# One of the two operands of each VectorE instruction of a state-space layer moved to PSUM, and the banks dealt out anew

## The chip, the cores and the metric

The kernel runs on one core of a Trainium2 chip. The metric is device time in microseconds (us) of one execution. Five engines work side by side, each through its own queue in order: PE (TensorE, matmuls), DVE (VectorE), ACT (ScalarE), POOL (GpSimd) and SP (SyncE, which here only issues DMAs). They meet at semaphores. SBUF is the on-chip memory of tiles; PSUM is a smaller one of eight banks, into which PE writes, and which DVE and ACT read and write too. In this kernel a bank is 128 x 512 float32, and every PSUM tile is called `b`.

## The reference

A decoder trunk over 256 tokens of 2048 channels in float32: one state-space (S5) layer and a SwiGLU, one dilated attention layer and a SwiGLU, each behind an RMS norm. Only the S5 part is touched:

```
dt = exp(log_dt);  mag = exp(lam_re * dt);  ang = lam_im * dt
lam = mag * (cos ang + i sin ang)                 # 128 groups x 64 states, complex
f   = (lam - 1) * conj(lambda) / |lambda|^2
x_t = lam * x_(t-1) + f * B u_t                   # a scan over the 256 tokens
y_t = Re(C x_t) + d_skip * u_t
z   = gelu(y);  out = val(z W) * sigmoid(gate(z W))
```

## The kernel before

**Two parts.** The first 188 us of the span are the S5 layer; the rest is a stream of large matmuls (lines 717, 718 and 721) over glu, the two SwiGLUs and attention, with PE as its bound. The stream begins when the last scan result has gone through PE.

**The S5 layer.** Tokens are taken in 64 chunks of four, the 128 groups in 64 pairs, and the pairs in four quarters k = 0 to 3 of 16 pairs. Its steps, in the order in which DVE meets them:

- Parameters (`s5_params`): some 72 small DVE instructions, mostly 128x64, one after another: exp of a step, sine and cosine by polynomials, the first four powers of lam (`by`, three instructions of `cmul` each), the coefficients of W. Operands and results lie in SBUF tiles (named `hi`, `lo` and `scr` here, since small vectors are packed in larger tiles).
- `s5_chunk_powers` on POOL: powers 1 to 4 of lam^4, in a small SBUF tile (`cp`).
- `w_build` on DVE: W for all quarters, 128x256 pieces with the coefficients `g` in PSUM bank 7. PE transposes them (`v_trans`), ACT copies them to `wpad`, PE multiplies with the tokens (`v_build`), ACT copies the result into `vs`, the 64 states per chunk.
- The scan over `vs` in three kinds of levels, each of the form dst += a^c * src: `l1` within blocks of four chunks (three levels of 128x512 or 128x480 instructions), `l2` across the 15 blocks for 32 pairs at once (14 steps of four 128x64 instructions, each step reading the one before), `l3` from the blocks to their chunks (three levels of 128x480). One level is four DVE instructions (lines 504 to 507): two products (of the state and of the state with its planes swapped), a sum, a sum back into `vs`. `pipe` sets the products of one level between the sums of the last, `go(ops, others)` spreads one list of instructions between another's.
- DVE's order: `l1([0, 1])`; `l2(0)` with `l1([2])` spread between; `l3(0)`; `l2(1)` with `l3(1)` spread between; `l3(2)`; half-size levels of quarter 3. POOL does `l1([3])`, the last level of quarter 3, and `q_build` (Q = C lam^t) in its own queue beside it.
- PE: `t_part(k)` (32 matmuls, the part of y that comes from the tokens of the same chunk) and `s_part(k)` (64 matmuls of line 581 onto the same banks, from the states), then ACT's gelu, then `z_part(k)`: eight transposes, an ACT copy (`hi` part) and two DVE subtractions (`lo` part) that give the stream its operand.

**What sets the order.** All of it is the order in which the program is written: each engine executes its instructions in that order, with semaphore waits that the framework derives from reads and writes of tiles. The products of the levels go to `t1p` (bank 6, and `za` or `hi` tiles in SBUF) and `dtmp` (SBUF); the coefficients come from `cp` in SBUF.

Of the kernel before, what the change touches and what calls it, by code (L numbers as in the profile page):

```python
# [32 lines left out]
def constants():  # L33
    """Identity, channel mask, selections of token rows, and the three attention masks."""
# [21 lines left out]
def layouts(i):  # L56
    """The inputs as the program reads them: copies in another order, nothing else."""
# [42 lines left out]
class Trunk:  # L100
# [50 lines left out]
    # ------------------------------------------------------------------ setup  # L151
# [39 lines left out]
    def s5_load(self):  # L191
# [7 lines left out]
        # planes of B: (Br, -Bi, -Br) times the gain; of C: (-Ci, Cr, Ci)  # L199
# [7 lines left out]
        # Q of two quarters of the pairs, a block for each g2: (slot, g2, t, c, re/im, q)  # L207
# [24 lines left out]
    def cmul(self, eng, out, ar, ais, x, xs, t1, t2):  # L232
        """out = a x for planes (re, im): ar twice, ais = (-im a, im a), xs = (im, re) of x."""
        eng.tensor_tensor(t1, ar, x, ALU.mult)
        eng.tensor_tensor(t2, ais, xs, ALU.mult)
        eng.tensor_tensor(out, t1, t2, ALU.add)

    def s5_params(self, rms):
        """Powers of the transition, and the coefficients of W."""
        nc, small = self.nc, self.small  # L240
# [16 lines left out]
        pio.append(lambda: tt(den, lr, lr, mul))  # L257
# [32 lines left out]

        tt(lam[:, 0, 1:3], bc(mag, S3, [1]), pp.rearrange("p (r q) -> p r q", r=2), mul)
# [4 lines left out]
        by(lam[:, 1:2, 1:3], lam[:, 0, 1], lam[:, 0, 2], lam[:, 0:1], 1)  # L296
        # f = (lam - 1) conj(lambda) / |lambda|^2
        u1, u2 = [v.rearrange("p (r q) -> p r q", r=2) for v in (ap_, az)]
        tt(u1, bc(lr, S3, [1]), nr[:, 0:2], mul)
        ts(lam[:, 1, 0], lam[:, 1, 2], -1.0, None, mul)  # L300
        tt(u2, bc(li, S3, [1]), nr[:, 1:3], mul)
        tt(u1, u1, u2, add)
        by(lam[:, 2:4, 1:3], lam[:, 1, 1], lam[:, 1, 2], lam[:, 0:2], 2)
        tt(fx, u1, bc(den, S3, [1]), mul)
# [5 lines left out]
        by(g[:, 2::-1], fx[:, 0], fx[:, 1], lam[:, 0:3], 3)  # L310

    def s5_chunk_powers(self, eng):
        """Powers 1..4 of conj(lam^4): re, and (im, -im) of conj, for the chunk recurrence."""
        mul = ALU.mult
        lam = self.lam
        sm = [self.small(w, True) for w in (192, 192, 128, 192, 192, 128)]
        cp = self.cp = [sm[i].rearrange("p (r q) -> p r q", r=3) for i in (0, 1, 3, 4)]
        tmp = self.ctmp = [sm[i].rearrange("p (r q) -> p r q", r=2) for i in (2, 5)]
        # plane 0: re; planes 1, 2: (b, -b) where a = re - i b
# [15 lines left out]
    def zv(self, k, hl):  # L335
        """A part of z^T of four K tiles."""
        c = 2048 * (k % 2) + 1024 * hl
        return self.zt[k // 2][:, c:c + 1024].rearrange("p (k t) -> p k t", k=4)

    def s5(self, st):  # L340
# [16 lines left out]
        # 1 / rms of the tokens: by rows, then for every (g2, j, c) in the partitions  # L357
# [5 lines left out]
        # B with the gain of u, conjugate  # L363
# [3 lines left out]
        # d_skip times the gain on the diagonal of the kernel of lag 0  # L367
# [44 lines left out]
        def q_build(k, ts):  # L412
            """Planes (re, im) of Q_t = C lam^t, t = 1..4, of 16 pairs."""
# [17 lines left out]
        def w_build(k, q0, n):  # L431
            """W_j = lam^(3-j) f B of n pairs (conjugate), in [(g2,p), q, re/im, j, c]."""
# [20 lines left out]
        def v_build(u):  # L453
            """The states that the chunks add, of 8 pairs."""
# [15 lines left out]
        def k_build(k):  # L470
            """K[3-j] = Re(C lam^(3-j) f B) of 16 pairs in [(k // 2, j, c), q, g2, c']."""
# [10 lines left out]
        def t_tile(t, n):  # L482
            """A blank tile for T of n pairs: (g2, j'), q, c'."""
# [5 lines left out]
        def t_build(t, h, bs):  # L489
            """T[j, j'] = K[j' - j]: the rows of K moved by 16 (3 - j') partitions, of 16 or 32 pairs."""  # L490
# [6 lines left out]
        def level(k, src, dst, ns, coef, eng, n, q0=0, nq=16):  # L497
            """slots dst += a^coef * slots src, nq pairs."""
# [5 lines left out]
            return [lambda: eng.tensor_tensor(ta, bc(cp[coef][:, 0, qs], sh, [1, 1]), x, mul),  # L504
                    lambda: eng.tensor_tensor(tb, bc(cp[coef][:, 1:3, qs], sh, [1]), x[:, :, ::-1, :], mul),  # L505
# [52 lines left out]
        # Y = U T + S Q, z = gelu(Y), transposed and split  # L558
# [561 lines left out]
```

## Time and profile before

| | |
|---|---|
| median of 3 timed runs | 2275.83 us (2275.25 to 2276.38) |
| span of the profiled execution | 2274.4 us |
| PE busy | 2157.1 us, 95% |
| DVE busy | 1591.5 us, 70% |
| ACT busy | 1034.1 us, 45% |
| POOL busy | 207.4 us, 9% |
| mean granted TensorE clock | 0.985 |

The span runs from the first to the last instruction of the profiled execution; it lies 1.4 us under the median of the timed runs. The shares are means over two unlike parts: in the S5 part (up to 188.4 us) DVE is busy for 175 us and PE for 89, and after it PE for nearly all of the time. "Held" in what follows means that an instruction's recorded time is longer than that of the same instruction elsewhere.

### The profile page before, as it was taken

To read this page: it belongs to the slowest core of one execution; us is meant where nothing else is said; L and a number is where in the kernel's file an instruction comes from. 1 tells how busy PE (TensorE), PEld (TensorE's weight loads), DVE (VectorE), ACT (ScalarE), POOL (GpSimd) and SP (SyncE) were. 2 spreads that over 40 slices of the span, in tenths; PEclk is the share of its full clock that TensorE was granted. 3 is DMA by queue.
4 is the path that set the end of the run, shared out by engine and by line. 5 is a ranking of instruction groups with operands and counts; after the bars stand their busy time and mean duration, and the time that the engine had idled before them with its cause. 6 is when DMAs were issued, how large, how long until landed. Compare 5 with 4: busy or idle time off the path is not lost.

```text
span 2274.4 us, 27357 instructions
## 1 busy us (share of the span) xinstructions
PE 2157.1 (95%) x10520; PEld 1793.2 (79%) x10520; DVE 1591.5 (70%) x2646; ACT 1034.1 (45%) x1173; POOL 207.4 (9%) x166
## 2 busy tenths in 40 slices
PE   2639999999999999999999999999999999999998
PEld 2628888888888888878888888887888888888886
DVE  9995677677677766484777677677776776675544
ACT  4503444544444444343545555545444444443443
POOL 7930000000000000000000000000000000000000
PEclk9869999999999999999999999999999999999999
DMA  5324545555555555545555444445555555555553
GB/s 183 90 84 163 189 185 193 209 191 185 204 185 191 199 196 192 200 173 199 195 185 184 146 154 166 148 167 185 187 191 199 194 192 199 189 204 203 194 195 130
DMA packets 60563, 410.37 MB, mean 180 GB/s; under 512 B 7248, under 2 KB 8144, under 8 KB 12816
## 3 DMA queue, kind: packets, MB, share of 16 engines
q1 hardware_dynamic: 58176, 400.13, 48.8%
q10 hardware_dynamic: 1968, 6.92, 0.9%
q8 instruction: 82, 1.34, 0.2%
q0 software_dynamic: 288, 1.57, 0.2%
q14 instruction: 49, 0.40, 0.0%
HBM read 398.90 MB, written 2.10 MB: 176 GB/s over the span
## 4 chain that ended last, share of the span: by engine, by line
PE 87%; DVE 10%; issue 1%; ACT 1%; DMA 0%; ACTq 0%; DVEq 0%
PE b L718 28%; PE b L717 28%; PE b L721 28%; DVE scr L787 2%; DVE scr L137 1%; DVE lo L137 1%; PE b L149 1%; DVE dtmp L505 1%; PE b L581 1%; DVE vs L507 1%; PE b L1010 1%; DVE vs L137 1%; ACT hi L695 1%; DVE raw L137 1%; PE b L1041 1%
## 5 line engine op out<-in xcount | busy, mean ns | idle before, releaser
L146 DVE SCALAR_TENSOR_TENSOR lo<-raw,gcol,hi 128x1024 fp32r<-128x1024 f32 x464 | 594.6, 1291 | 325.2 <-ACT hi L699 319.2
L717 PE MATMUL b<-hi,xt 128*128 128x512 f32 x1856 | 726.6, 391 | 1.5 <-ACT hi L699 1.3
L718 PE MATMUL b<-lo,xt 128*128 128x512 f32 x1856 | 723.1, 390 | 0.9 <-DVE lo L146 0.9
L699 ACT ACTIVATE hi<-raw,gcol 128x1024 fp32r<-128x1024 f32 x464 | 525.2, 1148 | 399.3 <-PE b L721 376.5
L721 PE MATMUL b<-hi,xt 128*128 128x512 f32 x1856 | 572.3, 390 | 0.0
L137 DVE TENSOR_TENSOR lo<-raw,hi 128x1024 fp32r<-128x1024 f32 x272 | 335.8, 1240 | 301.5 <-ACT hi L695 300.0
L695 ACT CAST hi<-raw 128x1024 fp32r<-128x1024 f32 x272 | 283.5, 1052 | 315.3 <-PE b L721 305.9
L717 PEld LDWEIGHTS b<-hi,xt 128*128 128x128 f32 x1856 | 349.0, 188 | 73.5 <-ACT hi L699 1.8
L718 PEld LDWEIGHTS b<-lo,xt 128*128 128x128 f32 x1856 | 348.9, 188 | 72.8 <-DVE lo L146 1.8
L721 PEld LDWEIGHTS b<-hi,xt 128*128 128x128 f32 x1856 | 348.7, 188 | 73.0
L718 PE MATMUL b<-lo,ht 128*128 128x512 f32 x704 | 274.3, 390 | 2.5 <-DVE lo L137 2.5
L717 PE MATMUL b<-hi,ht 128*128 128x512 f32 x704 | 274.0, 389 | 0.1
L787 DVE STREAM_TRANSPOSE scr<-scr 32x128 f32<-32x128 f32 x704 | 212.9, 302 | 11.3
L721 PE MATMUL b<-hi,ht 128*128 128x512 f32 x704 | 217.1, 389 | 0.0
L718 PEld LDWEIGHTS b<-lo,ht 128*128 128x128 f32 x704 | 132.2, 188 | 31.4 <-DVE lo L137 4.1
L717 PEld LDWEIGHTS b<-hi,ht 128*128 128x128 f32 x704 | 132.2, 188 | 27.8 <-ACT hi L695 0.5
L721 PEld LDWEIGHTS b<-hi,ht 128*128 128x128 f32 x704 | 132.2, 188 | 27.5
L791 POOL TENSOR_TENSOR ht<-scr,ht 128x512 fp32r<-128x512 f32 x44 | 57.1, 1297 | 880.8 <-ACT ht L790 852.4
L790 ACT CAST ht<-scr 128x512 fp32r<-128x512 f32 x44 | 27.3, 621 | 178.6 <-DVE scr L787 178.6
L791 POOL TENSOR_TENSOR xt<-scr,xt 128x512 fp32r<-128x512 f32 x20 | 25.9, 1297 | 830.6 <-ACT xt L790 725.2
L718 PE MATMUL b<-lo,z 128*128 128x512 f32 x256 | 100.1, 391 | 0.6 <-DVE lo L137 0.6
L787 DVE STREAM_TRANSPOSE scr<-x 32x128 f32<-32x128 f32 x320 | 96.8, 302 | 4.9
(210 smaller groups left out, 1605.0 us busy)
## 6 DMA issues: line engine op xcount, KB each, us to landing
raw<-in_fi SPq DMA_DIRECT2D x176, 1024.0 KB, 4.8
raw<-in_fo SPq DMA_DIRECT2D x88, 1024.0 KB, 4.8
raw<-in_wq SPq DMA_DIRECT2D x48, 1024.0 KB, 4.8
raw<-in_glu SPq DMA_DIRECT2D x32, 1024.0 KB, 4.8
raw<-in_wo SPq DMA_DIRECT2D x16, 1024.0 KB, 4.8
raw<-in_kv SPq DMA_DIRECT2D x8, 1024.0 KB, 4.8
qp<-in_xr SPq DMA_DIRECT2D x4, 512.0 KB, 11.0
xw<-in_xu SPq DMA_DIRECT2D x4, 512.0 KB, 11.5
```

What stands on the lines that cost most here:

```text
L137: self.nc.vector.tensor_tensor(out, in0, in1, op)
L146: self.nc.vector.scalar_tensor_tensor(out, in0, s, in1, op0, op1)
L149: self.nc.tensor.transpose(out, in_, self.ident[:n, :n])
L505: lambda: eng.tensor_tensor(tb, bc(cp[coef][:, 1:3, qs], sh, [1]), x[:, :, ::-1, :], mul),
L695: nc.scalar.copy(hi, raw)
L699: nc.scalar.activation(hi, raw, AF.Copy, scale=gk)
L717: nc.tensor.matmul(ps[b], xh, hi[:, c], start=first, stop=False)
L718: nc.tensor.matmul(ps[b], xh, lo[:, c], start=False, stop=False)
L721: nc.tensor.matmul(ps[b], xl, hi[:, c], start=False, stop=last)
L787: nc.vector.transpose(out[32 * q:32 * q + 32, :, 32 * a:32 * a + 32], src[32 * a:32 * a + 32, :, q, :])
L790: nc.scalar.copy(dst(0), out)
L791: nc.gpsimd.tensor_tensor(dst(1), out, dst(0).bitcast(F32), ALU.subtract)
```

## The change

The text of the program changes in the S5 functions alone. Parameters: `n, p, dt, mag, den, kk, app, pp, low, t1, nr, fx` move to PSUM banks 0 to 3 (`ps`), the others stay in SBUF; the two squares of |lambda|^2 go from DVE to ACT; |angle| is taken by two shifts in place of a minimum; two copies (`low`) are added. Chunk powers: `cp` stays in SBUF for POOL, and ACT copies it to two banks (`coefs`, banks 7 and 5), from which DVE reads. Products: `t1p` is banks 6 and 4 for all DVE levels; in `l2` the first product goes to the bank that holds the coefficients. Banks: `kk` takes 0 and 1, `t_part` 2 and 3 or 0 and 1, `z_part(0)` 7 and 2. Order: `t_part(2)` and `t_part(3)` come after `s_part(1)`, and the two subtractions of `z_part(0)` come before `l3(2)`.

```diff
+        homes = [[self.bank(i), 0] for i in (0, 1, 2, 3)]
+        ins = self.small
...
+        t, r = ins(64), ins(64)
+        n, p, dt, mag = [ps(64) for _ in range(4)]
+        zz, mags, k2, ang, l2, dens = [ins(64) for _ in range(6)]
+        den, kk = ps(64), ps(64)
+        ap_, az = ins(128), ins(128)
+        app, pp = ps(128), ps(128)
+        nc.scalar.activation(den, lr, AF.Square)
+        nc.scalar.activation(l2, li, AF.Square)
         for f in self.exp_steps(dt, ldt, t, n, r, p):
             f()
...
-        pio.append(lambda: tt(den, lr, lr, mul))
+        pio.append(lambda: tt(den, den, l2, add))
...
+        low = ps(256).rearrange("p (k r q) -> p k r q", k=2, r=2)
+        t1, t2 = ps(384), ins(384)
...
+        nc.vector.tensor_copy(low[:, 0], lam[:, 0, 1:3])
...
         def level(k, src, dst, ns, coef, eng, n, q0=0, nq=16):
...
-            return [lambda: eng.tensor_tensor(ta, bc(cp[coef][:, 0, qs], sh, [1, 1]), x, mul),
-                    lambda: eng.tensor_tensor(tb, bc(cp[coef][:, 1:3, qs], sh, [1]), x[:, :, ::-1, :], mul),
+            a_ = cp[coef][:, :, qs]
+            if eng is dve:
+                a_ = cps[k // 2][:, coef, :, 16 * (k % 2) + q0:16 * (k % 2) + q0 + nq]
+            return [lambda: eng.tensor_tensor(ta, bc(a_[:, 0], sh, [1, 1]), x, mul),
+                    lambda: eng.tensor_tensor(tb, bc(a_[:, 1:3], sh, [1]), x[:, :, ::-1, :], mul),
...
+        def coefs(h, b):
+
+            v = self.bank(b)
+            cps[h] = v[:, 0:384].rearrange("p (k r q) -> p k r q", k=4, r=3)
+            tl2[h] = [w.rearrange("p (r q) -> p r q", r=2) for w in (v[:, 384:448], self.ctmp[:, 64 * h:64 * h + 64])]
+            nc.scalar.copy(cps[h], self.cpa[:, :, :, 32 * h:32 * h + 32])
...
-            ta, tb = ta4[0][:, h], ta4[1][:, h]
+            ta, tb = tl2[h]
+            a_ = cps[h][:, 3]
...
-        t1p = [t1p[0], za[:, 1024:1536]]
+        coefs(0, 7)
+        coefs(1, 5)
         go(l1([0, 1], dve))
...
-        py = [t_part(0, tz, 32), t_part(1, tz, 32), t_part(2, tq[0], 16)]
+        py = [t_part(0, tz, 32), t_part(1, tz, 32)]
...
-        lo = z_part(0)
+        lo = z_part(0, (7, 2))
         l31 = l3(1)
         go(l2(1), l31)
-        py.append(t_part(3, tq[1], 16))
+        go(lo)
+        s_part(1, py[1])
+        py += [t_part(2, tq[0], 16), t_part(3, tq[1], 16)]
         next(st)
-        s_part(1, py[1])
...
         s_part(2, py[2])
-        go(lo)
```

DVE at the start of the parameters, before. `hi_84` is the tile of the inputs, `hi_108` that of small vectors, both in SBUF:

```order
L143 TENSOR_SCALAR hi_84<-hi_84 128x64 [waits DMAHW1_49]
L143 TENSOR_SCALAR hi_108<-hi_84 128x64 [waits DVE_49]
L141 TENSOR_SCALAR hi_108<-hi_108 128x64 [waits DVE_49] x2
L146 SCALAR_TENSOR_TENSOR hi_108<-hi_108,hi_84 128x64
L141 TENSOR_SCALAR hi_108<-hi_108 128x64 [waits DVE_49]
```

And of the changed kernel, where `b_129` is bank 0 of the parameters:

```order
L143 TENSOR_SCALAR hi_84<-hi_84 128x64 [waits DMAHW1_49]
L143 TENSOR_SCALAR hi_108<-hi_84 128x64 [waits DVE_49]
L141 TENSOR_SCALAR b_129<-hi_108 128x64 [waits DVE_49,Activation_49]
L141 TENSOR_SCALAR hi_108<-hi_108 128x64 [waits DVE_49]
L146 SCALAR_TENSOR_TENSOR hi_108<-b_129,hi_84 128x64
L141 TENSOR_SCALAR hi_108<-hi_108 128x64 [waits DVE_49]
```

The third instruction now writes to PSUM, and it has a wait on ACT that it did not have. What it waits for stands in ACT's queue of the changed kernel (L377 are the squares of the token rows, L393 the gain of B, L259 and L260 the two squares of |lambda|^2, the first into the same bank `b_129`):

```order
L377 ACTIVATE qp,ss<-qp 128x1024 [waits DMAHW7_49]
L393 ACTIVATE z_86<-z_86 128x16x64 [waits DMAHW3_49,Pool_49]
L259 ACTIVATE b_129<-hi_84 128x64 [waits DMAHW1_49]
L260 ACTIVATE hi_108<-hi_84 128x64
L398 ACTIVATE r<-r 128x2 [waits DVE_49]
```

The two squares stand behind all four row squares and the gain of B.

DVE where `l1` ends and `l2(0)` begins, before (`scr_106` and `scr_107` hold powers, `vs` the states, `b_242` is bank 6):

```order
L504 TENSOR_TENSOR b_242<-scr_106,vs 128x512 [waits Activation_49]
L137 TENSOR_TENSOR scr_107<-scr_107,vs 128x64 [waits DVE_49,Pool_49]
L137 TENSOR_TENSOR scr_107<-scr_107,vs 128x64 [waits Pool_49]
L137 TENSOR_TENSOR scr_107<-scr_107,vs 128x64 [waits DVE_49]
L137 TENSOR_TENSOR vs<-scr_107 128x2x32 [waits DVE_49]
L137 TENSOR_TENSOR scr_107<-scr_107,vs 128x64 [waits DVE_49]
```

And in the changed kernel, where `b_765` is bank 7 and `b_767` bank 5:

```order
L523 TENSOR_TENSOR b_250<-b_767,vs 128x512 [waits Activation_49]
L137 TENSOR_TENSOR b_765<-b_765,vs 128x64 [waits DVE_49]
L137 TENSOR_TENSOR scr_106<-b_765,vs 128x64 [waits DVE_49,Pool_49]
L137 TENSOR_TENSOR b_765<-b_765,vs 128x64 [waits DVE_49]
L137 TENSOR_TENSOR vs<-b_765,scr_106 128x2x32 [waits DVE_49]
L137 TENSOR_TENSOR b_765<-b_765,vs 128x64 [waits DVE_49]
```

Each instruction has one operand in a bank, and the second product of a step now waits for the first, since both name the same bank.

ACT of the changed kernel where the states are finished (L480 are the last copies of `v_build` into `vs`, L551 the copies of the coefficients into the banks, L501 the blank tile for `t_build`). In the kernel before, the L480 rows are L464, and the L501 rows (there L485) follow them directly:

```order
L480 COPY vs<-b_720 128x8x63 [waits PE_49]
L480 COPY vs<-b_738 128x8x63 [waits PE_49]
L648 DMA xw<-in_cd 128x1024 [waits DMAHW5_49,DMAHW1_49]
L551 COPY b_765<-scr_107 128x384 [waits DVE_49,Pool_49]
L551 COPY b_767<-scr_107 128x384
L501 COPY tz<-vs 128x2048 [waits Activation_49]
```

The copy that the first `l1` instruction reads (it has a wait on ACT) is the last but two of this list, behind every copy of `v_build`.

## Rows read from the trace of the kernel before

**Rows 1.** Stretches of the S5 layer, one row each: the stretch in us, its length, then for PE, weight loads, DVE, ACT and POOL the busy time and the instructions in brackets, then granted TensorE clock, DMA share and GB/s.

```profile
66.20:95.00 28.80, 25.92 (x486) 23.96 (x484) 28.77 (x25) 17.76 (x22) 28.01 (x19) 1.00 0.37 98
95.00:138.00 43.00, 4.57 (x48) 3.96 (x43) 42.16 (x70) 5.49 (x3) 33.65 (x26) 0.58 0.16 40
145.00:162.20 17.20, 11.53 (x110) 10.37 (x112) 16.44 (x68) 3.64 (x5) 0.00 (x0) 0.80 0.47 136
162.20:173.40 11.20, 7.11 (x62) 6.40 (x58) 11.10 (x14) 1.20 (x2) 6.30 (x4) 0.80 0.41 169
173.40:188.40 15.00, 14.99 (x128) 14.21 (x128) 8.92 (x20) 3.80 (x5) 0.00 (x0) 0.89 0.13 43
```

**Rows 2.** PE in order of time from `s_part(0)` to the first matmul of the stream; in brackets the idle time before and what ended it.

```profile
145.03 7.79 PE L581 MATMUL b<-qp,vs 128*64 128x128 f32 x64 [40.21 <-DVE vs L507]
...
154.10 1.97 PE L567 MATMUL b<-raw,xw 128*64 128x128 f32 x32
161.60 7.71 PE L581 MATMUL b<-qp,vs 128*64 128x128 f32 x64 [5.54 <-DVE vs L507]
173.41 7.79 PE L581 MATMUL b<-xw,vs 128*64 128x128 f32 x64 [4.11 <-DVE vs L507]
180.91 7.63 PE L581 MATMUL b<-qp,vs 128*64 128x128 f32 x64
188.47 0.50 PE L717 MATMUL b<-hi,z 128*128 128x512 f32 x1
```

**Rows 3.** The small instructions of `l2(0)`, grouped, from 95 to 138 us, with POOL busy for most of it: count, busy us and mean ns, idle before.

```profile
L137 DVE TENSOR_TENSOR scr<-scr,vs 128x64 f32<-128x64 f32 x42 | 22.3, 572 | 0.3
L137 DVE TENSOR_TENSOR vs<-scr 128x64 f32<-128x64 f32 x14 | 10.4, 742 | 0.4
```

**Rows 4.** The same of `l2(1)`, from 145 to 162.2 us, with POOL idle.

```profile
L137 DVE TENSOR_TENSOR scr<-scr,vs 128x64 f32<-128x64 f32 x42 | 7.4, 219 | 0.3
L137 DVE TENSOR_TENSOR vs<-scr 128x64 f32<-128x64 f32 x14 | 3.1, 224 | 0.4
```

**Rows 5.** POOL in order of time, early in `l1`: start, length, engine, line, operation, tiles (out<-in).

```profile
66.45 1.60 POOL L236 TENSOR_TENSOR hi<-lo 128x512 f32<-128x512 f32 x1
68.13 1.59 POOL L234 TENSOR_TENSOR lo<-scr,z 128x512 f32<-128x512 f32 x1
69.68 1.74 POOL L235 TENSOR_TENSOR lo<-scr,z 128x512 f32<-128x512 f32 x1
```

**Rows 6.** DVE in order of time beside POOL's rows of the group before.

```profile
66.85 1.75 DVE L505 TENSOR_TENSOR dtmp<-scr,vs 128x512 f32<-128x512 f32 x1
68.53 0.69 DVE L506 TENSOR_TENSOR b<-b,vs 128x512 f32<-128x512 f32 x1
69.13 1.14 DVE L504 TENSOR_TENSOR z<-scr,vs 128x512 f32<-128x512 f32 x1
70.19 0.68 DVE L507 TENSOR_TENSOR vs<-b,dtmp 128x512 f32<-128x512 f32 x1
```

**Rows 7.** ACT in order of time: the gain of B (line 377 before, 393 after).

```profile
16.02 1.04 ACT L377 ACTIVATE z<-z 128x1024 f32<-128x1024 f32 x1
```

**Rows 8.** DVE in order of time in the parameters, and the first instruction of `w_build` (last row).

```profile
6.43 2.03 DVE L141 TENSOR_SCALAR hi<-hi 128x64 f32<-128x64 f32 x2
8.38 0.22 DVE L146 SCALAR_TENSOR_TENSOR hi<-hi,hi 128x64 f32<-128x64 f32 x1
...
11.98 4.66 DVE L141 TENSOR_SCALAR hi<-hi 128x64 int32<-128x64 int32 x2
16.56 2.39 DVE L146 SCALAR_TENSOR_TENSOR hi<-hi 128x64 f32<-128x64 f32 x3
18.87 0.18 DVE L141 TENSOR_SCALAR hi<-hi 128x64 f32<-128x64 f32 x1
...
29.07 0.43 DVE L137 TENSOR_TENSOR b<-b,z 128x256 f32<-128x256 f32 x1
```

**Rows 9.** The last POOL instruction before the chunk powers (d_skip on the diagonal), beside the parameters.

```profile
16.94 1.92 POOL L371 TENSOR_TENSOR lo<-cst,hi 128x1024 f32<-128x1024 f32 x1
```

**Rows 10.** ACT in order of time where `v_build` ends: the last two copies into `vs`; in brackets the idle time before and what ended it.

```profile
74.73 1.96 ACT L464 COPY vs<-b 128x504 f32<-128x504 f32 x2 [0.36 <-PE b L460]
```

**Rows 11.** DVE in order of time at the start of `l3(2)`.

```profile
162.25 0.66 DVE L504 TENSOR_TENSOR hi<-scr,vs 128x480 f32<-128x480 f32 x1
162.82 1.65 DVE L505 TENSOR_TENSOR dtmp<-scr,vs 128x480 f32<-128x480 f32 x1
```

**Rows 12.** The first step of `l2(1)` in order of time (two products and a sum, the sum back into `vs`, the next product).

```profile
145.59 0.49 DVE L137 TENSOR_TENSOR scr<-scr,vs 128x64 f32<-128x64 f32 x3
146.11 0.23 DVE L137 TENSOR_TENSOR vs<-scr 128x64 f32<-128x64 f32 x1
146.37 0.23 DVE L137 TENSOR_TENSOR scr<-scr,vs 128x64 f32<-128x64 f32 x1
```

**Rows 13.** DVE instructions of 256 columns in order of time: two operands and the result in SBUF; one operand in a bank; the sum of two products, one of them in a bank.

```profile
25.72 0.42 DVE L236 TENSOR_TENSOR scr<-lo 128x256 f32<-128x256 f32 x1
...
29.41 0.41 DVE L137 TENSOR_TENSOR dtmp<-b,z 128x256 f32<-128x256 f32 x1
...
30.41 0.58 DVE L137 TENSOR_TENSOR raw<-b,dtmp 128x256 f32<-128x256 f32 x1
```

**Rows 14.** POOL in order of time: the last piece of `q_build`.

```profile
128.63 1.27 POOL L236 TENSOR_TENSOR raw<-z 128x512 f32<-128x512 f32 x1
```

More of the change, by code (lines that the diff above doesn't have):

```diff
@@ L238, in s5_params @@
     def s5_params(self, rms):
-        nc, small = self.nc, self.small
+        nc = self.nc
         tt, ts, stt = self.tt, self.ts, self.stt
@@ L243, in s5_params, with ps @@
         I = lambda v: v.bitcast(I32)
-        lr, li, ldt = self.par[:, 0:64], self.par[:, 64:128], self.par[:, 128:192]
-        t, n, r, p, dt, zz = [small(64) for _ in range(6)]
+        homes = [[self.bank(i), 0] for i in (0, 1, 2, 3)]
+        ins = self.small
+        def ps(w):
+            h = next(h for h in homes if h[1] + w <= 512)
+            h[1] += w
+            return h[0][:, h[1] - w:h[1]]
+        lr, li, ldt = self.par[:, 0:64], self.par[:, 64:128], self.par[:, 128:192]
+        t, r = ins(64), ins(64)
[6 more added lines that the diff above has]
+        nc.scalar.activation(l2, li, AF.Square)
         for f in self.exp_steps(dt, ldt, t, n, r, p):
             f()
-        mag = small(64)
         tt(zz, lr, dt, mul)
         e_ops = self.exp_steps(mag, zz, t, n, r, p)
-        ang, k2, kk = [small(64) for _ in range(3)]
-        ap_, az, pp = [small(128) for _ in range(3)]
-        den = small(64)
         pio = []
@@ L295, in s5_params @@
         nc.vector.tensor_copy(nr[:, 1], lam[:, 0, 2])
-        by(lam[:, 1:2, 1:3], lam[:, 0, 1], lam[:, 0, 2], lam[:, 0:1], 1)
-        u1, u2 = [v.rearrange("p (r q) -> p r q", r=2) for v in (ap_, az)]
+        by(lam[:, 1:2, 1:3], low[:, 0], lam[:, 0:1], 1)
+        u1, u2 = [v.rearrange("p (r q) -> p r q", r=2) for v in (app, az)]
         tt(u1, bc(lr, S3, [1]), nr[:, 0:2], mul)
         ts(lam[:, 1, 0], lam[:, 1, 2], -1.0, None, mul)
+        nc.vector.tensor_copy(low[:, 1], lam[:, 1, 1:3])
         tt(u2, bc(li, S3, [1]), nr[:, 1:3], mul)
         tt(u1, u1, u2, add)
-        by(lam[:, 2:4, 1:3], lam[:, 1, 1], lam[:, 1, 2], lam[:, 0:2], 2)
-        tt(fx, u1, bc(den, S3, [1]), mul)
+        by(lam[:, 2:4, 1:3], low[:, 1], lam[:, 0:2], 2)
+        tt(fx, u1, bc(dens, S3, [1]), mul)
         ts(lam[:, 2:4, 0], lam[:, 2:4, 2], -1.0, None, mul)
@@ L309, in s5_params @@
         nc.vector.tensor_copy(g[:, 3], fx)
-        by(g[:, 2::-1], fx[:, 0], fx[:, 1], lam[:, 0:3], 3)
+        by(g[:, 2::-1], fx, lam[:, 0:3], 3)
     def s5_chunk_powers(self, eng):
@@ L315, in s5_chunk_powers @@
         lam = self.lam
-        sm = [self.small(w, True) for w in (192, 192, 128, 192, 192, 128)]
-        cp = self.cp = [sm[i].rearrange("p (r q) -> p r q", r=3) for i in (0, 1, 3, 4)]
-        tmp = self.ctmp = [sm[i].rearrange("p (r q) -> p r q", r=2) for i in (2, 5)]
+        sm = [self.small(w, True) for w in (768, 128, 128)]
+        self.cpa = sm[0].rearrange("p (k r q) -> p k r q", k=4, r=3)
+        cp = self.cp = [self.cpa[:, i] for i in range(4)]
+        tmp = [v.rearrange("p (r q) -> p r q", r=2) for v in sm[1:]]
+        self.ctmp = sm[1]
         eng.tensor_copy(cp[0][:, 0:2], lam[:, 3, 1:3])
@@ L561, in t_part @@
         def t_part(k, tz, nq):
-            py = [self.bank(2 * (k % 3) + g2) for g2 in range(2)]
+            py = [self.bank(2 - 2 * (k % 2) + e) for e in range(2)]
             for e in range(2):
@@ L585, in s_part, with z_part @@
             zs[k] = z.rearrange("p j i g c -> p j (i g c)")
-        def z_part(k):
+        def z_part(k, bs=(7, 6)):
             zf, lo = zs[k], []
@@ L591, in z_part @@
             for e in range(2):
-                pt = self.bank(7 - e)
+                pt = self.bank(bs[e])
                 for j in range(4):
@@ L622, in s5 @@
                 q_build(u // 4, ((u - 1) % 4, u % 4))
-        t1p = [t1p[0], za[:, 1024:1536]]
+        coefs(0, 7)
+        coefs(1, 5)
         go(l1([0, 1], dve))
-        kk = [self.bank(4 + b) for b in range(2)]
+        kk = [self.bank(b) for b in range(2)]
         for b in range(2):
@@ L644, in s5 @@
         go(l2(0), l1([2], dve))
-        t1p = [stage[0][0][:, 512 * c:512 * c + 512] for c in range(2)]
         q_build(2, range(4))
```

31 lines of the change are left out of this document (15 added, 16 removed).

## The prediction

> **What bounds the kernel now.** I read the stretches first. In the S5 layer DVE is busy almost without a gap (28.77 of 28.80 us, 42.16 of 43.00), while PE has little to do between 95 and 138 us [rows 1]; the stream starts when the last `s_part` has ended, at 188.47 [rows 2]. So a microsecond that DVE saves before the last level is a microsecond of the whole, as long as DVE stays the one that is late. The stream behind it is not touched.
>
> Then I looked at why DVE is busy. The stretch 95 to 138 and the stretch 145 to 162.2 do the same work (70 and 68 instructions), but the first takes 43 us and has POOL at work for 33.65 of them, the second takes 17.2 with POOL idle [rows 1]. Grouped, the same 42 small instructions have a mean of 572 ns in the one and 219 in the other, the 14 sums 742 and 224 [rows 3, 4]. In order of time it can be seen what does it: at 66.85 a product of two SBUF tiles is recorded with 1.75 us and ends at 68.60, just after a POOL instruction has ended at 68.05; the sum behind it, with one operand in a bank, takes 0.69 although POOL runs from 68.13 to 69.72; so does the sum into `vs` at 70.19, 0.68 beside POOL's 69.68 to 71.42; the next product of two SBUF tiles, at 69.13, takes 1.14 and again ends after POOL has [rows 5, 6]. An instruction with two SBUF operands is held until the running POOL instruction ends, one with a bank among its operands is not, whether its result goes to a bank or to SBUF. The change gives each of them a bank, so I expect the hold to go. What it adds are two waits on ACT and some inside DVE.
>
> **The change part by part** (times of the profiled execution, span 2274.4; the runs' median is 1.4 more).
>
> *Parameters: a loss of 4.4 us.* The third DVE instruction now writes bank 0, where ACT's square of lam_re goes first, and that square stands behind ACT's gain of B, which ends at 16.02 + 1.04 = 17.06 [rows 7]. With some 0.2 for the square, DVE goes on at about 17.2, where it was at 6.43 [rows 8]. Its fourth instruction still reads and writes SBUF alone, as the pair at 6.43 which took 2.03 for two, so POOL's instruction of 16.94 to 18.86 [rows 9] holds it: 18.9. The rest ran in 11.98 - 8.38 = 3.6 us, then five instructions that were held from 11.98 to 18.87 and that cost some 0.7 without the hold, then 29.07 - 18.87 = 10.2 [rows 8]: 14.5 us. That gives 33.4, and two more instructions 33.5: `w_build` starts 33.5 - 29.07 = 4.4 late. The bounds: if the fourth isn't held, 2.8; if each of the 74 instructions costs 0.02 more for its bank, 5.9. I take 4.4. From here on everything is 4.4 later; `w_build` already has a bank in every product and keeps its length, so it ends at 66.2 [rows 1] + 4.4 = 70.6.
>
> *The copy of the coefficients: 11 us of waiting.* The first `l1` instruction now reads bank 7, which ACT fills behind its last copy into `vs`. That copy ended at 74.73 + 1.96 = 76.69 [rows 10], and as it is fed by `w_build` it moves to 81.1. The new copy (128x384, some 0.5 by the rate of the 128x504 ones) makes it 81.6. DVE stands still from 70.6 to 81.6, and all its later work is queued behind that wait. If that copy were early, nothing; so 0 to 11, and I take 11, since the order of ACT leaves no way round.
>
> *`l1([0, 1])`.* 24 instructions. Unheld they follow each other at 69.13 - 68.53 = 0.60 (512 columns) [rows 6] and 162.82 - 162.25 = 0.57 (480) [rows 11]: 16 x 0.60 + 8 x 0.57 = 14.2 us in place of 28.9. It ends at 95.8, where it ended at 95 [rows 1]: what the hold gives back here is spent on the two waits.
>
> *`l2(0)` with `l1([2])`.* Unheld, a step has taken 146.37 - 145.59 = 0.78 us [rows 12], of which the dependent ones 0.26 each and the second product, which waits for nothing, 0.13. In the changed kernel that product waits too, so all 56 cost 0.26 (14.5 us); the 12 large ones cost 0.57 to 0.6 (7.0), and each of them covers the 0.13 of one wait (-1.5): 20 us, I take 19.9, against 43 before [rows 1]. End: 115.7, before 138.
>
> *`l3(0)`* ran beside an idle POOL (between the second and the third stretch of [rows 1], 7.0 us) and keeps its length: 122.8. *`l2(1)` with `l3(1)`* keeps no hold to lose, and gets the waits: 19.9 for 17.2. End: 142.7, where it was 162.25 [rows 11]. So at this point 19.6 us are gained: 23 in `l2(0)`, 14.7 in `l1`, less 15.4 of waits and 2.7 of new dependences in `l2(1)`.
>
> *From there to the stream.* Before: 188.47 - 162.25 = 26.2, of which `l3(2)` 173.41 - 162.25 = 11.2 (the first of its held instructions takes 1.65, one unheld starts 0.57 after the one before [rows 2, 11]), then two `s_part` of 7.5 [rows 2]. After: `lo` 1.3 and `l3(2)` unheld 6.9 would have DVE ready 8.3 after this point; but PE runs `s_part(1)` (7.7, begun some 1.0 before the point) and only then two `t_part` of 1.97 [rows 2], so PE is ready at 10.7 and is the later one. With 15.1 for both `s_part` the stream starts at 25.8. So here the hold that goes is taken up by PE, and the gain is 0.4, with the moved subtractions at nothing because PE covers them (uncovered: 1.3).
>
> *What a bank costs.* Of 256 columns an instruction with a bank took 0.41 to 0.43 and one without 0.42 [rows 8, 13]. So between 0 and 0.02 us for each instruction. On the path are some 170 (24 + 68 + 12 + 68), 0 to 3.4 us; I take 1.2. Not shown in any row is a small dependent instruction that reads what the one before it wrote to the bank; Its nearest rows are the sum at 30.41, which reads two fresh results, one of them in a bank, and took 0.58 where its products took 0.41 to 0.43, so +0.16 [rows 13], and the sum into `vs` at 70.19, with 0.68 like any other of 512 columns, so 0 [rows 6]. For the 112 small ones that is 0 to 18 us. I keep 0: the sum at 30.41 writes another layout than it reads, and the row of the same line as the levels is the nearer one. [...]
>
> Sum: 19.6 + 0.4 - 1.2 = 18.8 us. 2274.4 - 18.8 = 2255.6, and 2275.8 - 18.8 = 2257.0 for the runs.
>
> POOL doesn't get in the way: its last `q_build` piece ended at 128.63 + 1.27 = 129.9 [rows 14]. Even 4.4 later and not faster, its result is 19 us ahead of `s_part(2)`, which now starts at 153.4.
>
> **The rivals.**
>
> *Banks are dear.* [...] For it: no row shows a small dependent instruction in a bank, and the sum of 0.58 [rows 13]. Against it: 0.41 to 0.43 with, 0.42 without [rows 8, 13], 0.69 and 0.68 at 512 [rows 6].
>
> *The waits are shorter.* If bank and SBUF are told apart such that DVE doesn't stand still at `l1`, or the square comes earlier, 4.4 + 11 = 15.4 come back: 2242, and half of that 2249. Against: the order of the changed kernel has both waits on ACT, and ACT's queue is in order; its copies into `vs` follow each other until 76.69 [rows 10]. For it: a copy that waits 0.36 us for PE there [rows 10] isn't bound by `w_build` alone, so not all of the 4.4 need pass through ACT.
>
> *PE or POOL becomes the bound earlier.* If `t_part(0)` and `t_part(1)`, which follow ACT's now later copies, end after `l3(0)`, or `s_part(1)` takes longer at a granted clock of 0.5, some 3 to 6 us of the gain go: 2260 to 2263. PE was idle 40 us before `s_part(0)` [rows 2], so the first isn't likely.
>
> *Slower.* The small steps of `l2` as a chain through one bank: a product is written to the bank that also holds the coefficients, the next instruction reads both, and so on 112 times. If each costs 0.17 us more than the 0.26, the 18.8 us are gone (112 x 0.17 = 19), and from there on it is slower: 2285 at 0.25. For it: the 0.16 of the sum at 30.41 [rows 13], and that all 56 wait for the one before, where before only 42 did. Against it: `b<-b,vs` of 512 columns costs 0.69, as the sum into `vs` [rows 6], and the next one starts 0.60 after it.
>
> *It doesn't do what it says.* If a bank among the operands were not enough, all levels would stay held, and the two waits alone would remain: 2275.8 + 15.4 = 2291. The rows of the hold speak plainly against it [rows 5, 6].
>
> **How the numbers follow.** Forecast as worked out, 2253 to 2261: 0.60. Dear banks, 2264 to 2268: 0.13. Shorter waits, 2242 to 2252: 0.12. PE or POOL earlier, 2260 to 2264: 0.08. The chain through a bank dear enough to end within 4.6 us of before (0.2%, about what a measurement of this kernel tells from no change): 0.03; slower: 0.03 for the chain, 0.01 for the hold that stays. Faster: 0.93, same 0.03, slower 0.04. The range takes the forecast, the upper half of the shorter waits and the dear banks: 2247 to 2268; the ends at 18 us of the small ones and at 2291 are left out.
>
> **What would show it.** Right: DVE instructions of 128x64 beside POOL at about 0.22, in the stretch of `l2(0)` about 20 us long; `w_build` starting at 33 to 34 behind an idle DVE of 10 us whose releaser is ACT; a second idle stretch of 11 us before the first level, released by ACT; `s_part(2)` behind a `t_part` and not behind DVE. Wrong: small instructions that start 0.3 or more apart (dear banks), a product beside POOL with 1.2 us or more (the hold stays), or no idle time before `l1`.

## The result, and the profile after

The changed kernel takes 2256.71 us (median of 4 runs, 2256.42 to 2258.23), the kernel before beside it 2276.11 (2275.25 to 2276.49): a ratio of 0.9918, 95% interval 0.9904 to 0.9932, so 19.4 us less. 2257.0 was forecast. The profiled execution spans 2255.0 us, 19.4 less than before.

The stretches of the S5 layer after, in the columns of [rows 1], cut where the levels begin: DVE's new idle stretch, `l1`, `l2(0)`, `l3(0)`, `l2(1)`, `l3(2)`, and the last two `s_part`:

```profile
72.50:83.40 10.90, 8.03 (x178) 6.49 (x174) 0.09 (x1) 10.35 (x16) 9.07 (x9) 1.00 0.45 111
83.40:97.70 14.30, 14.30 (x244) 13.88 (x242) 14.22 (x25) 5.78 (x7) 13.91 (x12) 1.00 0.42 112
97.70:118.10 20.40, 4.55 (x82) 4.31 (x80) 18.78 (x70) 9.36 (x6) 19.62 (x17) 0.69 0.35 85
118.10:125.10 7.00, 0.00 (x0) 0.00 (x0) 6.93 (x13) 0.00 (x0) 6.76 (x6) 0.50 0.00 0
125.10:145.20 20.10, 10.71 (x80) 9.71 (x81) 18.48 (x68) 2.37 (x4) 4.14 (x4) 0.67 0.37 106
145.20:153.50 8.30, 8.30 (x91) 8.04 (x90) 8.16 (x14) 1.20 (x2) 4.76 (x4) 0.92 0.00 0
155.20:170.10 14.90, 14.90 (x133) 14.09 (x128) 5.89 (x13) 3.79 (x5) 0.00 (x0) 1.00 0.47 175
```

`l2(0)` has POOL at work for 19.62 of its 20.40 us and takes as long as `l2(1)`, where POOL is nearly idle; before it was 43 against 17.2 [rows 1]. The small instructions of `l2(0)` after, grouped, which answer to [rows 3]:

```profile
L137 DVE TENSOR_TENSOR b<-b,vs 128x64 f32<-128x64 f32 x28 | 6.4, 229 | 0.7
L137 DVE TENSOR_TENSOR scr<-b,vs 128x64 f32<-128x64 f32 x14 | 3.1, 223 | 0.5
L137 DVE TENSOR_TENSOR vs<-b,scr 128x64 f32<-128x64 f32 x14 | 3.1, 222 | 0.4
```

222 to 229 ns beside POOL, against 572 and 742 before and 219 and 224 with POOL idle [rows 3, 4]: the hold is gone, and the bank costs 10 ns at most. In `l2(1)` after, with POOL nearly idle, the same three groups have 229, 223 and 223 ns, so POOL beside them makes no difference any more.

DVE after in order of time, the beginning of the parameters, the first instruction of `w_build`, and the first of `l1` (in brackets the idle time before and what ended it):

```profile
17.11 0.23 DVE L141 TENSOR_SCALAR b<-hi 128x64 f32<-128x64 f32 x1 [10.69 <-ACT b L259]
17.37 1.47 DVE L141 TENSOR_SCALAR hi<-hi 128x64 int32<-128x64 int32 x1
18.76 0.21 DVE L146 SCALAR_TENSOR_TENSOR hi<-b,hi 128x64 f32<-128x64 f32 x1
...
35.28 0.43 DVE L137 TENSOR_TENSOR b<-b,z 128x256 f32<-128x256 f32 x1
...
83.45 0.70 DVE L523 TENSOR_TENSOR b<-b,vs 128x512 f32<-128x512 f32 x1 [10.86 <-ACT b L551]
```

Both waits on ACT are there, 10.69 and 10.86 us, and `w_build` starts 6.2 us later than at 29.07 [rows 8]. The second row has one operand, in SBUF, and its result in SBUF: it ends at 18.84, just after POOL's instruction of that time (16.86 to 18.78), as forecast.

PE after, which answers to [rows 2]:

```profile
144.22 7.71 PE L608 MATMUL b<-qp,vs 128*64 128x128 f32 x64 [1.46 <-DVE vs L526]
151.67 3.76 PE L594 MATMUL b<-raw,xw 128*64 128x128 f32 x64
155.18 7.70 PE L608 MATMUL b<-xw,vs 128*64 128x128 f32 x64
162.59 7.63 PE L608 MATMUL b<-qp,vs 128*64 128x128 f32 x64
170.15 0.50 PE L744 MATMUL b<-hi,z 128*128 128x512 f32 x1
```

`s_part(2)` follows two `t_part` without a gap, while the last instruction of `l3(2)` had ended at 153.5: PE is the later one here. The stream starts at 170.15 in place of 188.47, which is 18.3 of the 19.4 us; the stream itself took 1.1 us less.

### The profile page after: what moved, and what is told of

Its sections match the earlier page's. It is cut to its first block, busy times and chain, and to the rows that moved or that the text cites. A ratio compares the mean times of both kernels' runs of the same rounds, so it can differ in the third digit from the quotient of the medians.

```text
span 2255.0 us, 27355 instructions
## 1 busy us (share of the span) xinstructions
PE 2154.6 (96%) x10520; PEld 1791.5 (79%) x10520; DVE 1546.1 (69%) x2648; ACT 1035.3 (46%) x1177; POOL 196.8 (9%) x166
## 4 chain that ended last, share of the span: by engine, by line
PE 88%; DVE 8%; issue 2%; ACT 1%; DMA 1%; SPq 0%; ACTq 0%; DVEq 0%
PE b L745 28%; PE b L744 28%; PE b L748 28%; DVE scr L814 2%; DVE lo L137 1%; PE b L608 1%; DVE b L137 1%; PE b L149 1%; PE b L1037 1%; ACT hi L722 1%; DMA qp<-in_xr 1%; DVE raw L137 1%; PE b L1068 1%; DVE b L523 0%; DVE b L525 0%
## 5 line engine op out<-in xcount | busy, mean ns | idle before, releaser
L744 PE MATMUL b<-hi,z 128*128 128x512 f32 x256 | 100.0, 391 | 0.0
```

Source lines behind the costliest of these rows:

```text
L744: nc.tensor.matmul(ps[b], xh, hi[:, c], start=first, stop=False)
```

## The experiments

All compared with the kernel before on the same chip, at 2275.3 to 2275.8 us; where a run is compared with the changed kernel, its median is set beside 2256.7. The kernel before had 2276.1 beside that one, so such a difference is uncertain by 0.3 to 0.8 us.

**The hold, from the changed kernel.** In `level` and `l2` the second product reads its coefficients from SBUF again:

```diff
-                    lambda: eng.tensor_tensor(tb, bc(a_[:, 1:3], sh, [1]), x[:, :, ::-1, :], mul),
+                    lambda: eng.tensor_tensor(tb, bc(cp[coef][:, 1:3, qs], sh, [1]), x[:, :, ::-1, :], mul),
...
-                        lambda x=x: tt(tb, a_[:, 1:3], x[:, ::-1, :], mul),
+                        lambda x=x: tt(tb, cp[3][:, 1:3, qs], x[:, ::-1, :], mul),
```

> Only the second product of each DVE level step reads its coefficients from SBUF again; first product, sums, waits and banks stay as changed. Theory (an instruction with two SBUF operands is held until the running POOL instruction ends): the second products beside POOL take 1.0 to 1.8 us in place of 0.22 to 0.69, the others stay at 0.22 to 0.69; l2(0) takes 30 to 37 us in place of 20.4, l1 17 to 22 in place of 14.2, l2(1) with POOL idle stays at 20; 2268 to 2278 us in all. Rival (the gain comes from somewhere else, for instance POOL no longer disturbed, or the products of a bank being cheap): second products stay under 0.8 us and the time stays within 4 us of 2256.7.

Measured: 2262.88 us, ratio to before 0.9945 (0.9928 to 0.9961), 6.2 slower than the changed kernel. Its stretches `l1`, `l2(0)` and `l2(1)`:

```profile
84.20:101.40 17.20, 17.20 (x298) 16.85 (x298) 17.17 (x24) 7.60 (x8) 16.81 (x13) 1.00 0.31 85
101.40:124.90 23.50, 1.58 (x28) 1.34 (x24) 22.73 (x69) 7.49 (x5) 22.64 (x18) 0.62 0.30 73
133.30:150.90 17.60, 10.35 (x78) 9.37 (x80) 16.81 (x69) 2.37 (x4) 1.24 (x1) 0.69 0.36 88
```

DVE in `l2(0)` in order of time:

```profile
102.83 0.22 DVE L137 TENSOR_TENSOR vs<-b,scr 128x64 f32<-128x64 f32 x1
103.09 0.23 DVE L137 TENSOR_TENSOR b<-b,vs 128x64 f32<-128x64 f32 x1
103.23 1.13 DVE L524 TENSOR_TENSOR dtmp<-scr,vs 128x512 f32<-128x512 f32 x1
104.28 1.28 DVE L137 TENSOR_TENSOR scr<-scr,vs 128x64 f32<-128x64 f32 x1
105.48 0.22 DVE L137 TENSOR_TENSOR b<-b,vs 128x64 f32<-128x64 f32 x1
```

And POOL beside it:

```profile
102.53 1.28 POOL L235 TENSOR_TENSOR z<-scr,z 128x512 f32<-128x512 f32 x1
103.88 1.59 POOL L236 TENSOR_TENSOR raw<-z 128x512 f32<-128x512 f32 x1
```

Only instructions that got their second SBUF operand back are held (1.28 until 105.56, just after POOL's 105.47), their neighbours stay at 0.22. The 14 small ones have a mean of 488 ns beside 223 and 226 of their neighbours, so not all are held as long: the one at 102.16 takes 0.50, until 102.66, where POOL's instruction of that time ends at 102.57. The theory of the hold stands, the rival doesn't; `l1` takes 17.2 as expected. But three numbers were missed. The time lies 5 us under the 2268 of the theory. `l2(0)` takes 23.5 and not 30 to 37: a held instruction waits for the rest of one POOL instruction, and where three unheld ones stand between two held ones, most of POOL's 1.3 us has passed by then. And `l2(1)` fell from 20.1 to 17.6, since the second product no longer names the bank that the first one writes, and so no longer waits for it: an effect of the edit that the expectation overlooked.

**The hold, from the kernel before.** DVE's instructions stay; POOL has less to do:

```diff
-        q_build(2, range(4))
...
-        q_build(3, range(4))
```

> The kernel before, with POOL's q_build of quarters 2 and 3 left out (so Q of these quarters isn't computed, and their part of y is not that of the reference); DVE's instructions are all as before, with two SBUF operands. Theory (the running POOL instructions hold them): l1 stays at 28.9 us, since q_build of quarters 0 and 1 and l1([3]) still run beside it; l2(0) falls from 42.9 us to 18 to 21, 2250 to 2254 us in all. Rival (the banks themselves make the levels faster, and POOL is not the cause): l2(0) stays above 35 us and the time above 2267.

Measured: 2251.82 us, ratio 0.9895 (0.988 to 0.991). Its stretches `l1` and `l2(0)`:

```profile
66.20:95.10 28.90, 25.99 (x491) 24.04 (x486) 28.87 (x25) 17.88 (x23) 28.12 (x19) 1.00 0.37 98
95.10:114.60 19.50, 4.72 (x50) 4.10 (x46) 18.74 (x69) 5.63 (x4) 2.69 (x2) 0.62 0.46 142
```

With POOL busy 28.12 us `l1` keeps its 28.9; with POOL busy only 2.69 `l2(0)` takes 19.5 in place of 43, without a single operand in another place. So it was POOL that made these instructions long.

**The parameters, taken out and put in alone.** First the changed kernel with `s5_params` as before, then the kernel before with the new `s5_params` and nothing else.

> The parameter steps alone are put back as before (vectors in SBUF, squares on DVE); coefficients, products and banks of the levels stay as changed. Theory (the parameter part only costs: 12.7 us of waiting for ACT's square and slower chains): w_build starts at 29.1 in place of 35.3, everything behind it comes 6.2 us earlier, 2250 to 2251 us. Rival (the wait for ACT's copy of the coefficients does not depend on w_build, so that it eats the 6 us): w_build starts earlier but l1 still starts at about 83.4 and the time stays at 2256 to 2257.

> The kernel before with the parameter steps of the changed kernel and nothing else. Theory (this part only costs: the wait for ACT's square and the waits in one bank): w_build starts 6.2 us later, and as l1 and l2(0) stay held by a POOL that is later too, 5 to 7 us are lost: 2281 to 2283. Rival (the held levels take the delay up, since POOL does not wait for all of it): 2276 to 2279.

Measured: without the new parameters 2252.02 us (2250.32 to 2252.16), 4.7 less than the changed kernel; with them alone 2281.04, ratio to before 1.0024 (1.0014 to 1.0034), 5.7 more than before. `w_build` starts at 29.14 in the first and at 35.06 in the second. So this part of the change is a loss of 4.7 and 5.7 us in the two surroundings, and the rest of the change alone is worth 23.8. In the first run the wait before `l1` was 11.78 us and not 10.86, and the stream took 2085.3 in place of 2084.8, which is why 4.7 and not 6.2 came through; the same 0.9 appear in other runs and are told of at the end.

**The first wait on ACT.** The squares go ahead of the gain of B and the row squares:

```diff
+        self.sqb, self.sql = self.bank(0), self.small(64)
+        nc.scalar.activation(self.sqb[:, 256:320], self.par[:, 0:64], AF.Square)
+        nc.scalar.activation(self.sql, self.par[:, 64:128], AF.Square)
         nc.scalar.activation(ngb, self.gb.rearrange("p (c q) -> p c q", c=16), AF.Copy, scale=-1.0)
...
-        nc.scalar.activation(den, lr, AF.Square)
-        nc.scalar.activation(l2, li, AF.Square)
```

> ACT's two squares of |lambda|^2 are put ahead of the gain of B and the squares of the token rows. Theory (DVE's third instruction waits for that square alone): the idle 10.7 us fall to 2 to 4, since ACT's table load ends at 8.1; some instructions that read and write SBUF alone are then held by POOL between 11.9 and 18.8; w_build starts at 28 to 30.5, 2250 to 2252 us. Rival (POOL's holds take what the wait gave): w_build starts at 33 or later, above 2254.

Measured: 2254.12 us, 2.6 less than the changed kernel. DVE in order of time:

```profile
8.50 0.23 DVE L141 TENSOR_SCALAR b<-hi 128x64 f32<-128x64 f32 x1 [2.10 <-ACT b L371]
...
11.73 2.45 DVE L143 TENSOR_SCALAR hi<-hi 128x64 f32<-128x64 f32 x2
...
14.56 1.93 DVE L141 TENSOR_SCALAR hi<-hi 128x64 int32<-128x64 int32 x1
...
16.80 2.02 DVE L141 TENSOR_SCALAR hi<-hi 128x64 int32<-128x64 int32 x2
...
30.98 0.43 DVE L137 TENSOR_TENSOR b<-b,z 128x256 f32<-128x256 f32 x1
```

The wait falls to 2.10 us, 8.6 less, but `w_build` comes only 4.3 earlier, later than the 28 to 30.5 expected: the chain now runs while POOL is busy, and its steps that only read and write SBUF take 2.45, 1.93 and 2.02 in place of 0.2 to 0.3. Neither theory had the numbers, but the rival named the cause: the wait had covered holds that come back without it. Another 1.0 of the gain went in the wait before `l1`, which is 11.83 in this run.

**The chains that share a bank.** On top of that edit, the vectors of the sine and of |lambda|^2 go to bank 1, away from those of the exponential:

```diff
-        homes = [[self.sqb, 0]] + [[self.bank(i), 0] for i in (1, 2, 3)]
+        homes = [[self.bank(0), 0], [self.sqb, 0]] + [[self.bank(i), 0] for i in (2, 3)]
...
+        homes[0][1] = 512
         den, kk = ps(64), ps(64)
...
-        self.sqb, self.sql = self.bank(0), self.small(64)
+        self.sqb, self.sql = self.bank(1), self.small(64)
```

> The squares first, as in the run of that edit, and the vectors of the sine and of |lambda|^2 in bank 1 in place of bank 0, apart from those of the exponential. Theory (in the changed kernel the two chains that are interleaved wait for each other, because they share a bank, and this is the 2 us by which the parameters are longer than forecast): w_build starts at 29.2 to 30.2 in place of 31.0, 2252.5 to 2253.5 us. Rival (the 2 us are the price of the operand in a bank): w_build starts at 30.8 to 31.2 and the time is that of the other run, 2254.1.

Measured: 2251.43 us (2250.1 to 2252.15), 2.7 less than without it, and `w_build` at 28.81: more than expected. Not all of that is the waits between the chains, since bank 0 no longer holds a square, and the third DVE instruction no longer waits for ACT at all; and 1.0 is the wait before `l1`, 10.87 here and 11.83 there. What is theirs can be seen in nine instructions that both kernels have in the same order (DVE in order of time in this run):

```profile
18.55 0.22 DVE L146 SCALAR_TENSOR_TENSOR b<-b,hi 128x64 f32<-128x64 f32 x1
18.69 0.21 DVE L275 COPY b<-hi 128x64 f32<-128x64 f32 x1
...
19.68 0.22 DVE L146 SCALAR_TENSOR_TENSOR b<-b,hi 128x64 f32<-128x64 f32 x1
```

and in the changed kernel:

```profile
24.68 0.23 DVE L146 SCALAR_TENSOR_TENSOR b<-b,hi 128x64 f32<-128x64 f32 x1
24.95 0.23 DVE L275 COPY b<-hi 128x64 f32<-128x64 f32 x1
...
26.60 0.23 DVE L146 SCALAR_TENSOR_TENSOR b<-b,hi 128x64 f32<-128x64 f32 x1
```

From the first to the ninth it is 19.68 - 18.55 = 1.13 us with two banks and 26.60 - 24.68 = 1.92 with one; the durations are the same, most of the starts lie 0.13 apart in place of 0.27. The run with the squares first, which still has one bank, takes 1.92 for them as well. So 0.8 us here are waits of instructions that have nothing to do with each other but the bank.

**The second wait on ACT.** The coefficients of the first half are copied early, to bank 5; those of the second half stay late, in bank 7:

```diff
         for u in range(8):
+            if u == 2:
+                coefs(0, 5)
...
-        coefs(0, 7)
-        coefs(1, 5)
+        coefs(1, 7)
...
-        lo = z_part(0, (7, 2))
+        lo = z_part(0, (5, 2))
```

> The copy of the coefficients of the first half is put in bank 5 and early in ACT's queue (between the copies of v_build), that of the second half in bank 7 where it was. Theory (the 10.9 us of idle DVE before l1 are only that copy's place in ACT's queue): l1 starts right behind w_build at 72.7 to 73.5, all levels come 10 to 11 us earlier, 2245 to 2247 us. Rival (what l1 or l2 reads, or POOL's l1([3]), is late by itself): idle time of 4 us or more shows before another level, and the time is 2250 or more.

Measured: 2246.18 us, ratio to before 0.9871 (0.9856 to 0.9885), 10.5 less than the changed kernel. DVE in order of time, the end of `w_build` and the start of `l1`:

```profile
71.36 1.04 DVE L137 TENSOR_TENSOR z<-b,dtmp 128x256 f32<-128x256 f32 x2
72.25 0.73 DVE L523 TENSOR_TENSOR b<-b,vs 128x512 f32<-128x512 f32 x1
```

There is no idle time left. The wait was only the place of one ACT copy in ACT's queue.

**The price of a bank, or a wait.** The first product of a step of `l2` goes to the other half's bank; each instruction has as many operands in banks as before the edit:

```diff
-            tl2[h] = [w.rearrange("p (r q) -> p r q", r=2) for w in (v[:, 384:448], self.ctmp[:, 64 * h:64 * h + 64])]
+            tl2[1 - h] = v[:, 384:448].rearrange("p (r q) -> p r q", r=2)
...
-        lo = z_part(0, (7, 2))
+        lo = z_part(0, (3, 2))
```

> The first product of each l2 step goes to the bank of the other half's coefficients, so that the second product no longer waits for the first; z_part(0) takes bank 3 in place of 7. Every instruction has the same operands in banks as before the edit. Theory (the 2.5 to 3 us that l2(1) is longer than in the kernel before are waits for one shared bank): l2(0) and l2(1) take 17.3 to 18.2 us each in place of 20.4 and 20.1, 2251 to 2252.5 us in all. Rival (they are the price of an operand in a bank): both stay at 20 us or more and the time stays at 2256 to 2257.

Measured: 2253.39 us, 3.3 less than the changed kernel. Its stretches `l2(0)` and `l2(1)`:

```profile
98.50:116.80 18.30, 4.58 (x83) 4.34 (x81) 17.30 (x70) 9.36 (x6) 17.67 (x15) 0.73 0.33 76
123.80:141.90 18.10, 9.58 (x78) 8.73 (x80) 16.99 (x68) 2.27 (x4) 6.26 (x5) 0.69 0.35 89
```

18.3 and 18.1 in place of 20.4 and 20.1: 4.1 us of the two `l2` were waits for a shared bank, and the rival is out. 0.8 of them were given back in the wait before `l1`, which is 11.70 in this run. They don't quite reach the 17.2 of [rows 1]; the large products now name the bank that the small steps write, and have a wait of their own (at 100.29 one starts 0.27 after the small one before it; in the changed kernel, at 99.53, it is 0.14).

**All together.** The four edits at once (`z_part(0)` in banks 3 and 2), and then the same levels with the parameter steps of the kernel before:

> Squares first, sine in its own bank, coefficients of the first half early in bank 5, first product of l2 in the other bank; z_part(0) takes bank 3. Theory (the four are on one chain and add): w_build at 29.5 to 30.2, l1 right behind it at 67, l3(2) 21 to 23 us earlier than in the changed kernel, 2233.5 to 2236.5 us. Rival (another engine takes over: ACT's copies into vs, POOL's q_build, or PE before s_part): idle time of 3 us or more on DVE before l2 or l3, 2238 us or more.

> As the run with all four edits, but with the parameter steps of the kernel before. Theory: w_build at 29.1, so 0.4 to 1 us earlier than with the squares first and the sine in its own bank; 2232.5 to 2236 us, the same as the other within 1.5 us. Rival (the parameters in banks are worth something once their waits are gone): 2 us or more slower than the other.

Measured: 2236.10 us (2235.49 to 2236.21), ratio to before 0.9826 (0.9811 to 0.9841), and 2235.83 (2235.14 to 2236.13), ratio 0.9825 (0.981 to 0.984). Both are 20.6 to 20.9 us faster than the changed kernel, and the same within what can be told. DVE of the first, two places in the parameters, their end, and the start of `l1`:

```profile
11.87 4.49 DVE L141 TENSOR_SCALAR hi<-hi 128x64 int32<-128x64 int32 x2
...
17.38 1.26 DVE L143 TENSOR_SCALAR hi<-hi 128x64 int32<-128x64 int32 x1
...
28.81 0.43 DVE L137 TENSOR_TENSOR b<-b,z 128x256 f32<-128x256 f32 x1
...
65.06 1.03 DVE L137 TENSOR_TENSOR z<-b,dtmp 128x256 f32<-128x256 f32 x2
65.95 0.74 DVE L526 TENSOR_TENSOR b<-b,vs 128x512 f32<-128x512 f32 x1
```

No idle time stands before `l1`, and `l2(0)` takes 18.2 us, with POOL at work for 17.65 of them. The parameters in banks are worth nothing here even with their waits gone: `w_build` starts at 28.81 with them and at 29.09 without. The first two rows show why: not every parameter step has a bank. Three integer steps that read and write SBUF alone are held by POOL, the last until 18.6, where the old steps were held until some 18.9.

## Why the prediction was right

**The hold.** The step that said that an instruction with two SBUF operands waits for the running POOL instruction, and one with a bank doesn't, is shown from three sides: by giving the second operand back (`l1` 14.2 to 17.2, the single instructions at 1.28), by taking POOL's work away (`l2(0)` 43 to 19.5), and by the trace after (222 to 229 ns beside POOL). `l1` was to take 14.2 us and took 97.68 - 83.45 = 14.2; `l2(0)` 19.9 and took 20.4; `l2(1)` 19.9 and took 20.1; `l3(0)` 7.0 and 7.0.

**The two waits on ACT.** Of the first, 17.2 was forecast for the third instruction and 17.11 measured; of the second, 11 us and 10.86. The edit that removes the second gave 10.5 us back. The 0.5 us for the copy doesn't follow from the 128x504 ones (1.96 for two would make some 0.75 for 384 columns); it came out right all the same, 0.98 for two.

**The parameters were mis-sized.** `w_build` was to start at 33.5 and started at 35.28. The step that failed is the one that took the 14.5 us of the old chain for the new one: it was 35.28 - 18.76 = 16.5. In `l2` I had counted that instructions that name one bank wait for each other; in the parameters, where exponential and sine are interleaved so that one runs while the other waits, I had not. 1.6 of the 2.0 us lie in that interleaved stretch: from 21.12 to 22.85 and from 23.56 to 28.51 in the changed kernel, 0.4 and 1.2 longer than the same parts before. Of these, 0.8 are shown to be such waits by the nine instructions, and 0.35 more by the first part, which takes 1.38 in the run with two banks (10.50 to 11.88) and 1.73 with one. The rest, with one added instruction in the second part, was not taken apart.

**The end.** From `l3(2)`'s turn to the stream 25.8 us were forecast; it was 170.15 - 145.2 = 25.0, with PE as the later one, as said. The two `t_part` took 3.5 together and not 3.9, and `s_part(1)` 7.45.

**The price of a bank.** 1.2 us were allowed for some 170 instructions. The small ones show 10 ns and less, the 512 ones 0.69 and 0.68 as before [rows 6]. Dependent steps in the bank start 0.26 apart, as in SBUF [rows 12]; in the changed kernel, from a sum into `vs` to the product that reads it:

```profile
99.13 0.22 DVE L137 TENSOR_TENSOR vs<-b,scr 128x64 f32<-128x64 f32 x1
99.39 0.23 DVE L137 TENSOR_TENSOR b<-b,vs 128x64 f32<-128x64 f32 x1
```

So the rival of the dear banks, and the slower one with its 0.17 us for each step of the chain, fall. No run shows a price of a bank that would make the 2264 to 2268 us of the first: the 128x64 instructions took 222 to 229 ns with a bank, 219 and 224 without [rows 4].

So the mechanism was right, but that 2257.0 came so near to 2256.7 is luck, by errors that cancel: 1.8 us too little for the parameters and 0.7 for the two `l2`, against 0.8 too much at the end, 1.2 for the banks, and 1.1 by which the stream was shorter. Nothing is to be read into the last: the stream took 2084.2 to 2085.9 us in the profiles of the twelve kernels of this document.

## What to carry to other kernels

In this kernel, where VectorE and GpSimd work side by side on SBUF, one operand in PSUM freed a VectorE instruction from the hold (128x64: 222 to 229 ns in place of 572 and 742), at no price that shows (219 and 224 with POOL idle); that, with the waits out of its way and the new order of PE's work, was worth 39.5 us (2275.3 to 2235.8), of which the change as it was made got 19.4. But in the waits a bank counted as one thing (10.69 us for ACT's square in bank 0, 4.1 in the two `l2`, 0.8 in the parameters): look what stands ahead of the instruction that fills it in that engine's queue (10.86 us before `l1`), and give chains that should overlap, and coefficients and results, a bank each. That, and leaving the parameters in SBUF or freeing them of their waits, was the other half.

## What the runs showed of the hardware that was not expected

A hold cost the rest of the running POOL instruction, not a fixed time: of the small second products of the first experiment the one at 102.16 took 0.50 us and the one at 104.28 took 1.28, and they ended 0.09 after POOL's instruction both times. With one small instruction in four open to it, `l2(0)` took 23.5 us where `l2(1)`, with POOL busy for 1.24, took 17.6, with all of them open to it 43 where it took 17.2. POOL paid too, where a wide DVE instruction with two SBUF operands ran on into POOL's next one: in the first experiment L524, held from 103.23, ended at 104.36, 0.55 after POOL's instruction of 102.53, and POOL's next one took 1.59 in place of 1.28. In `l1` before, with wide held instructions all along, POOL's took 1.59 to 1.74 [rows 5]. A small held one cost POOL nothing that shows: beside the sum into `vs` at 100.33 in the kernel before, held for 1.31, POOL's instruction took 1.27.

The wait before `l1` was 10.86 us in the changed kernel and 10.87 with the sine in its own bank, but 11.70 to 11.83 in four runs (11.78 without the new parameters) whose edits don't touch ACT's copies or PE's matmuls of `v_build`. What differs is PE's clock after a pause in `v_trans`. Stretches of the changed kernel there, columns as in [rows 1]:

```profile
54.00:58.00 4.00, 4.00 (x58) 3.67 (x60) 3.96 (x7) 2.82 (x5) 3.84 (x4) 0.57 0.02 4
58.00:62.00 4.00, 3.64 (x94) 3.27 (x88) 3.97 (x6) 3.82 (x6) 3.84 (x4) 1.00 0.70 158
```

and of the first experiment:

```profile
54.00:58.00 4.00, 4.00 (x52) 3.67 (x53) 3.96 (x7) 2.67 (x5) 3.84 (x4) 0.50 0.02 4
58.00:62.00 4.00, 4.00 (x92) 3.71 (x90) 3.96 (x6) 3.33 (x5) 3.84 (x4) 0.85 0.71 175
```

After 3.20 us of idle PE the changed kernel has a granted clock of 0.57 in these four microseconds and is back at 1.00 in the next; the experiment, after 3.87 us of idle, has 0.50 and then 0.85. The run with the sine in its own bank, after 3.19 us of idle, has 0.57 from 48 to 52 us and then 1.00. From the first of the eight transposes behind that pause to the first of the next eight, with 64 matmuls of `v_build` between, it is 4.55 us in the changed kernel and 4.53 with the sine in its own bank, but 5.48 in three of the four runs with the long wait: the first experiment, the one without the new parameters and the one with the squares first (the last two after 3.59 and 3.60 us of idle). PE feeds ACT there, and ACT's last copy is what `l1` waits for. That the clock is the whole of the 0.9 us was not tested.
